# Attention operands split once and kept in DRAM, the pool half's output projection moved into attention, the mask of the row maxima done by a matmul: one transformer block on one core

## The chip, the cores and the metric

The kernel runs on one core of a Trainium2 chip. The metric is the device time of one execution in microseconds (us). The engines are TensorE (PE in the rows; its weight loads are PEld), VectorE (DVE), ScalarE (ACT), GpSimd (POOL) and SyncE (SP), which issues most DMAs. Each engine runs its own instructions in order and waits on semaphores for the others.

## The reference, cut to what matters

One block over 16 meta tokens and 1024 frames (L = 1040 positions, width 1024, all float32):

```python
n1 = _rmsnorm(h, norm1_w)
proj = n1 @ w_in                                   # q, k, v (512 each), fg (8), u (512)
q = _rmsnorm(q per head of 64, q_norm_w); k = _rmsnorm(k per head, k_norm_w)
cum_logf = cumsum(log_sigmoid(fg + b_fgate))
# 8 heads, causal: logit[t, s] = q_t.k_s / 8 + cum_logf[t] - cum_logf[s], softmax, times v
a_out = _forgetting_attention(q, k, v, cum_logf)
# pool half: per group of 128 channels, mean over a trailing window minus the value itself
p_out = einsum(pooled, w_pool) * pool_scale
h = h + concat([a_out, p_out]) @ w_out
h = h + (silu(n2 @ w_gate) * (n2 @ w_up)) @ w_down   # n2 = _rmsnorm(h); width 2816
```

## The kernel before

Everything is held transposed: channels on the 128 partitions, positions along the columns, in chunks of 512 or 346 columns, one PSUM bank of the eight for each product. To keep float32 accuracy with a fast matmul, each operand is split into a high part (a rounded copy) and a low part (the rest), and each product is three matmuls: high by high, low by high, high by low. A split is one copy on ACT and one subtraction on DVE or POOL.

The stages on TensorE are: k of the first pair of heads and the gates while x arrives; v (`v_mm`, `v_evac`); the projections of q, k and u in the order of the list `order`, the last of them q of the fourth pair of heads, whose matmuls end at 220.9 us; the four pool maps (`pool_map`, tile pm, 24 matmuls); the output projection of the pool half (16 jobs of 12 matmuls, tile o, `out_job`); attention, heads 0 to 7; the attention half of the output projection; the SwiGLU (tiles gu and d), which takes the second half of the time. The program is written out in the order in which each engine is to run it: a manual schedule, in which lambdas in queues (`later`, `bg`, `fill_q`, `mq`, `behind`) are taken out at fixed points.

What the projections leave for attention is q, k and v in float32 (tiles q32, k32, v32). For each head, `stack` makes four operands Q1, Q2, K1, K2 that hold high and low parts one above the other in two halves of 64 partitions: ACT copies the high halves, SP moves some of them to the other half of the partitions by DMA, DVE makes the low halves (L625, L629). `vsplit` splits v of one head: ACT copies, POOL subtracts (L647). Both are strung out over the steps of the head before, through `bg`.

In attention a unit is a head and one of two blocks of 512 queries. Its row maxima are taken first (`mx_steps`, tile s, lines 675 to 681): two matmuls, and a reduction on DVE; where a chunk crosses the diagonal, DVE adds the mask and reduces in one instruction (L678), which in the trace is two, the second a read of the accumulator. `mt` turns the four maxima into rows of Q2: three small DVE instructions (L693 to L695), four transposes on TensorE (tile mt, L700) and a copy on ACT. Then come 3 or 7 steps (`sp_steps`): `front` (tile st, two matmuls and, on the diagonal, a third of 128 columns with a mask, L734; then Exp twice on ACT), `mid` (the low part of the weights, on POOL or every fourth on DVE), and three steps later `back` (tile pv). For heads 1 to 3 and the first two blocks of keys, `back` multiplies unsplit float32 weights with unsplit v (tile vd, L761, `DIRECT`). `MAXN` says in which steps the next unit's maxima are taken, two at a time. `FILL` says how much of an output job is put between steps: nothing in heads 0 to 3, where all 16 pool jobs are done before, then 11/40 and 14/40 a step of the jobs that multiply the first two pairs of heads (6 matmuls each).

Of the kernel before, what the change touches and what calls it, by code (L numbers as in the profile page):

```python
# [7 lines left out]
FT = mybir.dt.float32  # L8
# [32 lines left out]
ND, DIRECT = 2, (1, 2, 3)  # L41
AGE = 2
FILL = [0] * 8 + [11 / 40] * 6 + [14 / 40] * 2
# [3 lines left out]
def block_kernel(ctx, tc, hT, n1w, w_f, w_v, w_u, w_qk, b_f, qnw, knw, w_pool, pscale, w_out, n2w, w_g, w_up, w_d, outT):  # L47
# [56 lines left out]
    maskB = const([128, 512], FT, "maskB")  # L104
    G.memset(maskB, 0.0)
    G.affine_select(maskB[:, 384:], maskB[:, 384:], pattern=[[-1, 128]], compare_op=OP.is_ge, fill=-BIG, base=0, channel_multiplier=1)
# [134 lines left out]
    v32 = [ut(1024, FT, "v32") for _ in range(5)]  # L241
# [14 lines left out]
    def v_evac(j, p):  # L256
        sz = min(128, L - 128 * j)
        A.activation(v32[j // 2][:sz, 512 * (j % 2):512 * (j % 2) + 512], p[:sz], AF.Copy, scale=rcol[:sz, j:j + 1])
# [28 lines left out]
    q32, k32 = [None] * NP, [None] * NP  # L287
    later = []

    def qk_evac(p, n, cols, w, out):  # L290
# [5 lines left out]
        def rest():  # L296
# [20 lines left out]
    k32[0] = ut(L, FT, "k32")  # L317
    for (o, n), p in zip(CH3, k0_ps):
        qk_evac(p, n, slice(o, o + n), kw, k32[0][:, o:o + n])
# [119 lines left out]
    for x, (c, i) in enumerate(order):  # L439
        if x + 2 < len(order):  # L440
            staged.append(load_w(x + 2))
        if c == "u":
            t = ut(L, FT, "u")
        else:
            t = ut(L if c == "k" else SEQ, FT, c + "32")
            (k32 if c == "k" else q32)[i] = t
        if x + 1 == len(order):
# [20 lines left out]
            for p, (o, n) in zip(pb, CHQ):  # L468
                qk_evac(p, n, slice(o, o + n), qw, t[:, o - META:o - META + n])
            break  # L470
        for o, n in CHQ if c == "q" else CH3:
# [8 lines left out]
            else:  # L480
                a = o - META if c == "q" else o
                qk_evac(p, n, slice(o, o + n), kw if c == "k" else qw, t[:, a:a + n])
# [67 lines left out]

    def fill(n):
        while n and fill_q and fill_q[0][0] <= len(split_done):
            fill_q.pop(0)[1]()
            n -= 1

    def out_job(x, b, p=None):
# [11 lines left out]
        V.tensor_tensor(h2[m][:, S], p, h2[m][:, S], op=OP.add)  # L568
# [13 lines left out]
    vhb = []  # L582
    for i in range(2):
        vhb.append([ut(192 * nj, FR, "vh").rearrange("p (j c) -> p j c", c=192) for nj in (5, 4)])
        for t, nj in zip(vhb[i], (5, 4)):
            V.tensor_copy(t[:, :, 64:128], onesf[:, None, 0:64].to_broadcast([128, nj, 64]))

    vd = ut(1024, FT, "vd").rearrange("p (i j c) -> p i j c", i=2, j=4)
    V.tensor_copy(vd[:, :, :, 64:128], onesf[:, None, 0:64].to_broadcast([128, 8, 64]).rearrange("p (i j) c -> p i j c", i=2))
# [6 lines left out]
    SE = V  # L596

    def stack(h):

        q, k = q32[h // 2], k32[h // 2]  # L600
        dma = nc.sync.dma_start
        T, B = slice(0, 64), slice(64, 128)
        R, O = (T, B) if h % 2 == 0 else (B, T)
        t = []

        def start():
            t.extend([ut(SEQ, FR, "Q1"), ut(SEQ, FR, "Q2"), ut(L, FR, "K1"), ut(L, FR, "K2")])
            dma(f(t[1])[64:66], f(KAT[0])[4 * h + 2:4 * h + 4, :SEQ])
            dma(f(t[3])[64:68], f(KAT[0])[4 * h:4 * h + 4])

        def kc(o, n):
            C = slice(o, o + n)
            A.activation(t[2][R, C], k[R, C], AF.Copy)
            dma(f(t[3])[T, C], f(t[2])[R, C])
            if h % 2:
                dma(f(t[2])[T, C], f(t[2])[B, C])

        def qc(o, n):
            C = slice(o, o + n)
            A.activation(t[0][R, C], q[R, C], AF.Copy)  # L620
            dma(f(t[0])[O, C], f(t[0])[R, C])

        def ql(o, n):
            C = slice(o, o + n)
            SE.tensor_tensor(t[1][T, C], q[R, C], f(t[0])[R, C], op=OP.subtract)  # L625

        def kl(o, n):
            C = slice(o, o + n)
            SE.tensor_tensor(t[2][B, C], k[R, C], f(t[2])[R, C], op=OP.subtract)  # L629
            if o:  # L630
                heads[h] = tuple(t)

        bg.extend([start, lambda: kc(0, 520), lambda: kc(520, 520), lambda: qc(0, 512), lambda: qc(512, 512),
                   lambda: ql(0, 512), lambda: kl(0, 520), lambda: ql(512, 512), lambda: kl(520, 520)])

    def vsplit(h):
        for j, a, e in ((0, 0, 2), (2, 0, 2), (4, 0, 1), (5, 1, 2), (6, 0, 2), (8, 0, 1)):
            def piece(j=j, a=a, e=e):
                sz = min(128, L - 128 * j)
                src = v32[j // 2].rearrange("p (a c) -> p a c", c=512)[:sz, a:e, 64 * h:64 * h + 64]  # L640
                t, J = vhb[h % 2][j // 5], slice(j % 5, j % 5 + e - a)
                if h in DIRECT and j < ND:
                    A.activation(vd[:, h % 2, j:j + 2, 0:64], src, AF.Copy)
                    if j < 2:
                        return
                A.activation(t[:sz, J, 0:64], src, AF.Copy)
                G.tensor_tensor(t[:sz, J, 128:192], src, f(t)[:sz, J, 0:64], op=OP.subtract)  # L647
            bg.append(piece)
# [10 lines left out]
    def mx_steps(h, b):  # L659
# [5 lines left out]
        for a in range(4):  # L665
# [40 lines left out]
    def sp_steps(h, b):  # L706
# [9 lines left out]
        def direct(js):  # L716
            return h in DIRECT and js[-1] < ND

        def front(js, g):

            p = ps("st")
            p32, ph = ut(512, FT, "p32"), None if direct(js) else hs(512, FR, "ph")
# [18 lines left out]
            for sz, o0, o1 in g["parts"]:  # L741
                if ph is not None:
                    A.activation(ph[:sz, o0:o1], p[:sz, o0:o1], AF.Exp)
                A.activation(p32[:sz, o0:o1], p[:sz, o0:o1], AF.Exp)  # L744

        def mid(g, sub):
            if g["ph"] is None:
                return
# [5 lines left out]
        def back(js, g):  # L754
# [3 lines left out]
            if g["ph"] is None:  # L758
                j, = js
                lo, c0 = cols_of(j)  # L760
                mm(pv[:, c0:], vd[:, h % 2, j], g["p32"][:, :512 - c0], start=j == 0, stop=False)  # L761
                return
# [63 lines left out]
    background(4)  # L826
    vsplit(0)
    for _ in range(7):
        fill(1)
        background(2)  # L830
    stack(1)
    for s in mx_steps(*units[0]):
# [639 lines left out]
```

## Time and profile before

| | us |
|---|---|
| three runs, median (lowest to highest) | 1150.87 (1149.77 to 1151.78) |
| the profiled execution: its time | 1152.16 |
| the profiled execution: its span, first to last instruction | 1150.4 |
| TensorE busy | 1118.7 |
| VectorE busy | 759.6 |
| ScalarE busy | 486.0 |
| GpSimd busy | 382.9 |
| TensorE's last matmul of the q, k and u projections starts | 220.7 |
| first step of attention starts | 277.5 |
| attention's last step ends | 453.6 |

The timeline's starts of successive matmuls tell what a matmul costs in a stream (0.23 us for 512 columns); the durations beside them overlap. Idle time of an engine is put down to the instruction that ended it. The granted clock is the share of TensorE's full clock.

### The profile page before, as it was taken

How to read it: one execution, taken by the hardware profiler on the slowest of the kernel's cores; microseconds unless marked ns; L12 is line 12 of the kernel's file. 1: busy time of each engine (PE TensorE's matmuls, PEld its weight loads, DVE VectorE, ACT ScalarE, POOL GpSimd, SP SyncE). 2: the span in 40 equal slices, each digit the busy share in tenths (PEclk: the TensorE clock that was granted, in tenths of full speed). 3: DMA queues.
4: the chain of work that ended last, by engine and by line, in shares of the span. 5: the costliest groups of instructions: out<-in, count | busy, mean ns of one | idle time of the engine just before them, and what ended most of it. 6: DMA issues, size and time to landing. Idle time of an engine off the chain costs nothing.

```text
span 1150.4 us, 14601 instructions
## 1 busy us (share of the span) xinstructions
PE 1118.7 (97%) x5251; PEld 920.8 (80%) x5251; DVE 759.6 (66%) x1237; ACT 486.0 (42%) x907; POOL 382.9 (33%) x329
## 2 busy tenths in 40 slices
PE   7999999999999999898999999999999999999998
PEld 6778899787877788676888888888888888888886
DVE  7454753774788886899554455455535569778986
ACT  7343421632778675543423232223222335344542
POOL 0011244142436565639454345434543410000000
PEclk9999999999999999998999999999999999999999
DMA  7101110251021123320322132313231479643452
GB/s 241 56 19 37 37 56 10 66 167 46 20 49 34 25 56 102 119 101 5 106 86 98 40 107 74 110 37 110 74 105 42 154 260 357 203 141 101 157 191 110
DMA packets 48407, 112.45 MB, mean 98 GB/s; under 512 B 6560, under 2 KB 9120, under 8 KB 48336
## 3 DMA queue, kind: packets, MB, share of 16 engines
q1 hardware_dynamic: 38512, 95.23, 25.3%
q10 hardware_dynamic: 9824, 16.30, 3.8%
q8 instruction: 41, 0.67, 0.2%
q14 instruction: 30, 0.25, 0.1%
HBM read 86.10 MB, written 19.92 MB: 92 GB/s over the span
## 4 chain that ended last, share of the span: by engine, by line
PE 82%; DVE 12%; ACT 3%; issue 2%; DMA 1%; POOL 0%; SPq 0%; ACTq 0%; DVEq 0%; POOLq 0%
PE gu L1140 11%; PE gu L1141 11%; PE gu L1139 11%; PE d L1381 6%; PE d L1380 6%; PE d L1379 6%; PE pj L417 3%; PE pj L418 3%; PE pj L419 3%; PE o L516 2%; PE o L518 2%; PE o L517 2%; PE v L251 2%; PE v L252 2%; PE v L253 2%
## 5 line engine op out<-in xcount | busy, mean ns | idle before, releaser
L1140 PE MATMUL gu<-cb,ws 128*128 128x512 f32 x560 | 222.2, 397 | 4.1 <-DVE ws L1130 4.1
L1141 PE MATMUL gu<-cb,ws 128*128 128x512 f32 x560 | 221.9, 396 | 0.0
L1139 PE MATMUL gu<-cb,ws 128*128 128x512 f32 x560 | 221.5, 396 | 0.0
L1130 DVE TENSOR_TENSOR ws<-wst,ws 128x512 fp32r<-128x512 f32 x120 | 97.7, 815 | 125.3 <-ACT ws L1129 125.3
L1140 PEld LDWEIGHTS gu<-cb,ws 128*128 128x128 f32 x560 | 105.9, 189 | 29.6 <-DVE ws L1130 4.5
L1129 ACT ACTIVATE ws<-wst 128x512 fp32r<-128x512 f32 x120 | 69.9, 621 | 139.5 <-POOL wst L1124 130.9
L1139 PEld LDWEIGHTS gu<-cb,ws 128*128 128x128 f32 x560 | 105.9, 189 | 25.0
L1141 PEld LDWEIGHTS gu<-cb,ws 128*128 128x128 f32 x560 | 106.0, 189 | 24.7
L1381 PE MATMUL d<-hd,wd 128*128 128x512 f32 x308 | 121.3, 394 | 0.0
L1380 PE MATMUL d<-hd,wd 128*128 128x512 f32 x308 | 121.3, 394 | 0.0
L1379 PE MATMUL d<-hd,wd 128*128 128x512 f32 x308 | 121.2, 393 | 0.0
L1153 POOL TENSOR_TENSOR e<-e,e 128x512 f32<-128x512 f32 x20 | 29.6, 1479 | 159.6 <-DVE e L1166 106.9
L752 POOL TENSOR_TENSOR pl<-p,ph 128x512 fp32r<-128x512 f32 (+4 forms) x58 | 64.5, 1124 | 45.6 <-ACT p L744 43.3
L304 POOL TENSOR_TENSOR s<-t,g 128x346 f32<-128x346 f32 (+2 forms) x20 | 21.8, 1096 | 154.3 <-ACT g L303 143.6
L417 PE MATMUL pj<-xh,wh 128*128 128x346 f32 (+2 forms) x216 | 72.9, 337 | 0.0
L418 PE MATMUL pj<-xh,wl 128*128 128x346 f32 (+2 forms) x216 | 72.9, 337 | 0.0
L419 PE MATMUL pj<-xl,wh 128*128 128x346 f32 (+2 forms) x216 | 72.8, 337 | 0.0
L1380 PEld LDWEIGHTS d<-hd,wd 128*128 128x128 f32 x308 | 57.9, 188 | 13.5
L1379 PEld LDWEIGHTS d<-hd,wd 128*128 128x128 f32 x308 | 57.9, 188 | 13.5
L1381 PEld LDWEIGHTS d<-hd,wd 128*128 128x128 f32 x308 | 57.9, 188 | 13.3
L1068 ACT ACTIVATE hd<-wst 128x512 fp32r<-128x512 f32 x77 | 48.0, 623 | 36.3 <-issue 28.9
L1069 DVE TENSOR_TENSOR hd<-wst,hd 128x512 fp32r<-128x512 f32 x77 | 52.9, 687 | 9.6 <-ACT hd L1068 9.6
(291 smaller groups left out, 2528.2 us busy)
## 6 DMA issues: line engine op xcount, KB each, us to landing
wst<-in_w_d SPq DMA_DIRECT2D x77, 256.0 KB, 2.7
wst<-in_w_g SPq DMA_DIRECT2D x22, 512.0 KB, 6.2
wst<-in_w_up SPq DMA_DIRECT2D x22, 512.0 KB, 3.4
wst<-hidd SPq DMA_DIRECT2D x22, 512.0 KB, 7.3
wst<-in_w_d SPq DMA_DIRECT2D x11, 512.0 KB, 5.0
hidd<-e ACTq DMA_DIRECT2D x20, 256.0 KB
h<-in_hT SPq DMA_DIRECT2D x8, 512.0 KB, 7.6
h2d<-h SPq DMA_DIRECT2D x16, 256.0 KB, 2.0
```

Source lines behind the costliest of these rows:

```text
L417: mm(p[:, :n], wh[:, W], xh[k][:, o:o + n], start=k == 0, stop=False)
L418: mm(p[:, :n], wl[:, W], xh[k][:, o:o + n], start=False, stop=False)
L419: mm(p[:, :n], wh[:, W], xl[k][:, o:o + n], start=False, stop=k == KT - 1)
L752: sub.tensor_tensor(pl[:sz, o0:o1], p32[:sz, o0:o1], f(ph)[:sz, o0:o1], op=OP.subtract)
L1129: A.activation(t[:, :512], src, AF.Copy)
L1130: E.tensor_tensor(t[:, 512:], src, f(t)[:, :512], op=OP.subtract)
L1139: mm(p, w[:, W], c[:, :512], start=k == 0, stop=False)
L1140: mm(p, w[:, Wl], c[:, :512], start=False, stop=False)
L1141: mm(p, w[:, W], c[:, 512:], start=False, stop=k == 3)
L1379: mm(p, w[:, W], h[:, LO], start=i == 0, stop=False)
L1380: mm(p, w[:, Wl], h[:, LO], start=False, stop=False)
L1381: mm(p, w[:, W], h[:, HI], start=False, stop=i == NPR - 1)
```

## The change

- q and k (`qk_evac`): when a chunk is finished, ACT makes its high part (`high`), a step later DVE its low part (`low`), for both heads of a pair at once; the last chunk's `low` stores both tiles in DRAM (`qkd`). `v_evac` splits v straight from PSUM, with a block of ones between high and low, and stores it (`vsd`).
- `stack` is eight DMAs on SP's queue that load Q1, Q2, K1, K2 of a head, six of them 64 partitions high (256 KB), and `vload` is three that load its v. The splits within attention, and `vd` with the unsplit products, are gone.
- The mask of the maxima is a matmul of the identity with a 128x128 mask between the other two; DVE reduces without it.
- The output jobs of the pool half: two among the maxima of the first unit, one behind them, two in a ramp before the loop, the other 11 in the steps of heads 0 to 3 (`FILL` 12/40). The attention jobs follow at 16/40 a step. The addition of a job's result to h2 (DVE) waits in `post` until the next `flush`.
- The four pool maps are interleaved with the last steps of q's and k's normalization and splits (`run_later` between them), and the maxima of the first unit come right behind them.

```diff
-FILL = [0] * 8 + [11 / 40] * 6 + [14 / 40] * 2
+RAMP = 2
+FILL = [12 / 40] * 8 + [16 / 40] * 8
...
+                def high():
+                    A.activation(th[:, C], out, AF.Copy)
+
+                    def low():
+                        V.tensor_tensor(tl[:, C], out, f(th)[:, C], op=OP.subtract)
+                        if C.stop == width:
+                            for a, x in enumerate((th, tl)):
+                                nc.sync.dma_start(qkd[name][i, a, :, :width], f(x))
+                    later.append(low)
+                later.append(high)
...
+            A.activation(t[:sz, :, 0:64], src, AF.Copy, scale=rcol[:sz, j:j + 1])
+            V.scalar_tensor_tensor(t[:sz, :, 128:192], src, rcol[:sz, j:j + 1], f(t)[:sz, :, 0:64], op0=OP.mult, op1=OP.subtract)
+            nc.sync.dma_start(vsd[j, :sz, 768 * i:768 * i + 768], f(t)[:sz].rearrange("p h c -> p (h c)"))
...
+        for t, P, src in ((Q1, T, q[0]), (K1, T, k[0]), (Q1, B, q[0]), (K1, B, k[1]), (Q2, T, q[1]), (K2, T, k[0])):
+            dma(f(t)[P], src)
...
                     mm(p[:, :n], Q1[:, T], K1[:, o:o + n], start=True, stop=False)
+                    if last:
+                        mm(p[:, n - 128:n], ident, maskB, start=False, stop=False)
                     mm(p[:, :n], Q2[0:66, T], K2[0:66, o:o + n], start=False, stop=True)
-                    if last:
-                        V.tensor_tensor_reduce(p[:, :n], p[:, :n], maskB[:, 512 - n:], 1.0, -3e38, OP.add, OP.max,
-                                               accum_out=mp[:, a, c:c + 1])
-                    else:
-                        V.tensor_reduce(mp[:, a, c:c + 1], p[:, :n], op=OP.max, axis=AX.X)
+                    V.tensor_reduce(mp[:, a, c:c + 1], p[:, :n], op=OP.max, axis=AX.X)
...
+    stack(0)
+    vload(0)
     for g in (3, 2, 1, 0):
         pool_map(g)
-    stack(0)
-    for x in range(2):
-        fill(1)
-        background(3)
         now, later[:] = later[:], []
         run_later(now)
+    s0 = mx_steps(*units[0])
+    for x, s in enumerate(s0):
+        s()
+        if x % 2:
+            fill(1)
+            now, later[:] = later[:], []
+            run_later(now)
...
-    for _ in range(5):
+    for _ in range(RAMP):
         fill(1)
-        max_next(1)
-    max_next(2)
+        max_next(2)
```

ScalarE at the pool maps, before. mph is the high part of a pool map, g the reciprocal root of the last q chunks, K1 and Q1 head 0's operands:

```order
L501 ACTIVATE mph_325_1950<-pm_327_1952,psc_101 128x512
L501 ACTIVATE mph_325_1950<-pm_328_1958,psc_101 128x512
L501 ACTIVATE mph_329_1964<-pm_331_1966,psc_101 128x512
L501 ACTIVATE mph_329_1964<-pm_332_1972,psc_101 128x512
L501 ACTIVATE mph_333_1978<-pm_335_1980,psc_101 128x512
L501 ACTIVATE mph_333_1978<-pm_336_1986,psc_101 128x512
L501 ACTIVATE mph_337_1992<-pm_339_1994,psc_101 128x512
L501 ACTIVATE mph_337_1992<-pm_340_2000,psc_101 128x512
L545 ACTIVATE wo_344_2024<-wos_324_1948 128x512
L613 ACTIVATE K1_347_2029<-k32_67_482 64x520 x2
L302 ACTIVATE g_351_2041<-t_350_2040 128x512
L303 ACTIVATE g_351_2041<-g_351_2041 128x512
```

The same place in the changed kernel; kh and qh are the high parts of the last k and q:

```order
L529 ACTIVATE mph_346_2077<-pm_349_2085,psc_103 128x512
L330 ACTIVATE kh_284_1814<-k32_283_1813 128x346
L320 ACTIVATE g_352_2097<-t_351_2096 128x512
L321 ACTIVATE g_352_2097<-g_352_2097 128x512
L320 ACTIVATE g_356_2107<-t_355_2106 128x512
L321 ACTIVATE g_356_2107<-g_356_2107 128x512
L529 ACTIVATE mph_358_2113<-pm_360_2115,psc_103 128x512
L529 ACTIVATE mph_358_2113<-pm_361_2121,psc_103 128x512
L529 ACTIVATE mph_362_2136<-pm_364_2138,psc_103 128x512
L529 ACTIVATE mph_362_2136<-pm_365_2144,psc_103 128x512
L330 ACTIVATE qh_309_1938<-q32_308_1937 128x512 x2
L529 ACTIVATE mph_366_2152<-pm_368_2154,psc_103 128x512
```

The first map's parts stand where they stood; behind them now come the four instructions on g, and the last map's parts stand behind qh, which reads the finished q.

TensorE at the end of the same place in the changed kernel, from the last pool map on; s is a maximum of unit (0, 0), o the first output job:

```order
L528 MATMUL pm_369_2160<-wl_327_2028,wh_322_2001 128x512
L666 MATMUL s_371_2172<-K1_344_2064,Q1_342_2062 128x144
L668 MATMUL s_371_2172<-maskB_86,ident_69 128x128
L669 MATMUL s_371_2172<-K2_345_2065,Q2_343_2063 128x144
L666 MATMUL s_372_2177<-K1_344_2064,Q1_342_2062 128x272
L668 MATMUL s_372_2177<-maskB_86,ident_69 128x128
L669 MATMUL s_372_2177<-K2_345_2065,Q2_343_2063 128x272
L544 MATMUL o_375_2186<-mph_346_2077,wo_339_2055 128x512
L545 MATMUL o_375_2186<-mph_346_2077,wo_339_2055 128x512
L546 MATMUL o_375_2186<-mpl_347_2078,wo_339_2055 128x512
```

Before, the first o stood right behind the last pm, with the second q chunk's sums of squares (ss) behind it:

```order
L500 MATMUL pm_340_2000<-wl_309_1910,wh_304_1883 128x512
L516 MATMUL o_343_2010<-mph_325_1950,wo_322_1943 128x512
L517 MATMUL o_343_2010<-mph_325_1950,wo_322_1943 128x512
L518 MATMUL o_343_2010<-mpl_326_1951,wo_322_1943 128x512
L516 MATMUL o_343_2010<-mph_329_1964,wo_322_1943 128x512
```

In both kernels the last three matmuls of an o job read the last map's mph and mpl. In the changed kernel the ss matmuls stand between the first map and the second.

## Rows read from the trace of the kernel before

**Rows 1.** The page: busy time, share of the span and instructions by engine.
```profile
PE 1118.7 (97%) x5251; PEld 920.8 (80%) x5251; DVE 759.6 (66%) x1237; ACT 486.0 (42%) x907; POOL 382.9 (33%) x329
```
**Rows 2.** Stretches of one head each: length; PE, PEld, DVE, ACT, POOL busy; clock; DMA.
```profile
300.65:320.60 19.95, 19.28 (x113) 15.66 (x111) 17.15 (x41) 16.40 (x38) 9.49 (x12) 1.00 0.15 35
...
409.16:432.80 23.64, 21.90 (x129) 18.26 (x127) 21.71 (x46) 17.19 (x39) 14.92 (x19) 1.00 0.26 72
```
**Rows 3.** PE groups, 276.4 to 453.6: count | busy, mean ns | idle before, releasers.
```profile
L732 PE MATMUL st<-Q,K 128*128 128x512 f32 (+4 forms) x112 | 42.0, 375 | 0.7 <-DVE a L791 0.4 <-DVE mp L681 0.2
...
L675 PE MATMUL s<-K,Q 128*128 128x456 f32 (+6 forms) x103 | 34.0, 336 | 2.3 <-DVE a L791 1.8 <-DVE mp L678 0.4 <-ACT p L744 0.2
...
L700 PE MATMUL mt<-ident,Mc 128*68 128x128 f32 x60 | 7.0, 239 | 5.9 <-DVE Mc L695 3.2 <-DVE mp L663 1.1 <-ACT p L744 0.9
```
**Rows 4.** PE timeline, start and duration: a pair without mask; a pv triple, a masked pair.
```profile
287.37 0.39 PE L732 MATMUL st<-Q,K 128*128 128x512 f32 x1
...
287.83 0.35 PE L675 MATMUL s<-K,Q 128*128 128x400 f32 x1
...
316.11 0.40 PE L770 MATMUL pv<-ph,vh 128*128 128x512 f32 x1
...
316.82 0.39 PE L732 MATMUL st<-Q,K 128*128 128x512 f32 x1
317.05 0.21 PE L734 MATMUL st<-maskA,ident 128*128 128x112 f32 x1
317.10 0.45 PE L735 MATMUL st<-Q,K 68*128 68x512 f32 x1
317.39 0.32 PE L675 MATMUL s<-K,Q 128*128 128x346 f32 x1
```
**Rows 5.** PE timeline: an unsplit product (vd), the pair behind it, and what follows.
```profile
303.64 1.02 PE L761 MATMUL pv<-p,vd 128*128 128x512 f32 x2
...
304.97 0.23 PE L675 MATMUL s<-K,Q 128*128 128x144 f32 x1
```
**Rows 6.** DVE, ACT and POOL groups by form, 220.7 to 256 us: the pool maps.
```profile
L502 DVE SCALAR_TENSOR_TENSOR mpl<-pm,psc,mph 128x512 fp32r<-128x512 f32 x8 | 5.3, 736 | 0.0
L307 DVE SCALAR_TENSOR_TENSOR s<-s,g 128x512 f32<-128x512 f32 x2 | 2.5, 1254 | 0.0
...
L309 DVE SCALAR_TENSOR_TENSOR q<-pj,qw,g 128x512 f32<-128x512 f32 x2 | 1.5, 752 | 0.1
...
L501 ACT ACTIVATE mph<-pm,psc 128x512 fp32r<-128x512 f32 x8 | 5.0, 722 | 1.0 <-PE pm L500 1.0
...
L304 POOL TENSOR_TENSOR s<-t,g 128x512 f32<-128x512 f32 x2 | 2.6, 1304 | 3.0 <-ACT g L303 3.0
```
**Rows 7.** Timeline at the pool maps: DVE's last sum of squares, PE's maps.
```profile
222.51 0.69 DVE L294 TENSOR_TENSOR sql<-sq,sqh 128x512 fp32r<-128x512 f32 x1 [0.29 <-ACT sq L293]
...
220.91 0.39 PE L498 MATMUL pm<-wh,wh 128*128 128x512 f32 x1
...
226.43 0.50 PE L498 MATMUL pm<-wh,wh 128*128 128x512 f32 x1 [1.19 <-DVE mpl L502]
```
**Rows 8.** PE timeline: the longest wait in attention, and matmuls soon after it.
```profile
281.79 0.43 PE L700 MATMUL mt<-ident,Mc 128*68 128x128 f32 x4 [2.40 <-DVE Mc L695]
...
284.14 0.63 PE L771 MATMUL pv<-ph,vh 128*64 128x512 f32 x1
284.56 0.63 PE L772 MATMUL pv<-pl,vh 128*128 128x512 f32 x1
```
**Rows 9.** DVE groups by form, 276.4 to 453.6 us: work that the change removes.
```profile
L629 DVE TENSOR_TENSOR K<-k,K 64x520 fp32r<-64x520 f32 x12 | 10.3, 856 | 2.0 <-DMA K<-K 1.8
...
L625 DVE TENSOR_TENSOR Q<-q,Q 64x512 fp32r<-64x512 f32 x12 | 9.7, 809 | 4.9 <-ACT Q L620 4.6
...
L678 DVE DVE_READ_ACCUMULATOR2_ANT mp<- 128x1 f32 x58 | 8.0, 138 | 0.1
```
**Rows 10.** DMA issues: size of each, median us from issue to landing.
```profile
res<-h2d SPq DMA_DIRECT2D x16, 256.0 KB, 2.8
```

More of the change, by code (lines that the diff above doesn't have):

```diff
@@ L238, in block_kernel @@
         A.activation(fgT[:16, o:o + n], fg_ps[c][:16, :n], AF.Copy)
-    v32 = [ut(1024, FT, "v32") for _ in range(5)]
+    vst, vsd = [], DR.tile([ST, 128, 192 * NH], FT, name="vsd")
     rcol = const([128, ST], FT, "rcol")
@@ L284, in block_kernel, with qk_tile, qk_evac @@
         V.tensor_scalar(qrow[:, o:o + n], p[:, :n], 1.0 / D, EPS, op0=OP.mult, op1=OP.add)
-    q32, k32 = [None] * NP, [None] * NP
+    qkd = {c: DR.tile([NP, 2, 128, L], FT, name=f"{c}d") for c in "qk"}
     later = []
-    def qk_evac(p, n, cols, w, out):
+    def qk_tile(c, i):
+        n = L if c == "k" else SEQ
+        return c, i, n, ut(n, FT, c + "32"), ut(n, FR, c + "h"), ut(n, FR, c + "l")
+    def qk_evac(p, n, cols, w, tile, C):
+        name, i, width, t32, th, tl = tile
+        out = t32[:, C]
         h, l, s = hs(n, FR, "sqh"), hs(n, FR, "sql"), hs(n, FT, "sq")
@@ L444, in block_kernel @@
         else:
-            t = ut(L if c == "k" else SEQ, FT, c + "32")
-            (k32 if c == "k" else q32)[i] = t
+            t = qk_tile(c, i)
         if x + 1 == len(order):
@@ L481, in block_kernel @@
                 a = o - META if c == "q" else o
-                qk_evac(p, n, slice(o, o + n), kw if c == "k" else qw, t[:, a:a + n])
+                qk_evac(p, n, slice(o, o + n), kw if c == "k" else qw, t, slice(a, a + n))
             run_later(now)
@@ L549, in block_kernel, with flush @@
     wo = {}
+    post = []
+    def flush():
+        while post:
+            post.pop(0)()
     def fill(n):
         while n and fill_q and fill_q[0][0] <= len(split_done):
+            flush()
             fill_q.pop(0)[1]()
@@ L578, in out_fill @@
             fill_q.extend([(need, lambda x=x: out_job(x, 0)), (need, lambda x=x: out_job(x, 1))])
[L582 to L589, printed above, removed]
+    vhb = [[ut(192 * nj, FR, "vh").rearrange("p (j c) -> p j c", c=192) for nj in (5, 4)] for _ in range(2)]
     Mc = [const([128, 4, 68], FR, f"Mc{i}") for i in range(2)]
@@ L594, in block_kernel @@
     heads = {}
-    SE = V
     def stack(h):
-        q, k = q32[h // 2], k32[h // 2]
         dma = nc.sync.dma_start
         T, B = slice(0, 64), slice(64, 128)
[L603 to L648, printed above, removed]
+        R = (T, B)[h % 2]
@@ new lines, in stack, with vload @@
+        Q1, Q2, K1, K2 = heads[h] = ut(SEQ, FR, "Q1"), ut(SEQ, FR, "Q2"), ut(L, FR, "K1"), ut(L, FR, "K2")
+        q, k = [[qkd[c][h // 2, a, R, :n] for a in range(2)] for c, n in (("q", SEQ), ("k", L))]
+        for t, P, src in ((Q1, T, q[0]), (K1, T, k[0]), (Q1, B, q[0]), (K1, B, k[1]), (Q2, T, q[1]), (K2, T, k[0])):
+            dma(f(t)[P], src)
+        dma(f(Q2)[64:66], f(KAT[0])[4 * h + 2:4 * h + 4, :SEQ])
+        dma(f(K2)[64:68], f(KAT[0])[4 * h:4 * h + 4])
+    def vload(h):
+        for t, j, n, sz in ((0, 0, 5, 128), (1, 5, 3, 128), (1, 8, 1, 16)):
+            o = j - 5 * t
+            nc.sync.dma_start(f(vhb[h % 2][t])[:sz, o:o + n], vsd[j:j + n, :sz, 192 * h:192 * h + 192].rearrange("j p c -> p j c"))
@@ L714, in cols_of @@
             return lo, max(lo, 0)
-        def direct(js):
-            return h in DIRECT and js[-1] < ND
         def front(js, g):
             p = ps("st")
-            p32, ph = ut(512, FT, "p32"), None if direct(js) else hs(512, FR, "ph")
+            p32, ph = ut(512, FT, "p32"), hs(512, FR, "ph")
             g["p32"], g["ph"], g["parts"] = p32, ph, []
@@ L741, in front @@
             for sz, o0, o1 in g["parts"]:
-                if ph is not None:
-                    A.activation(ph[:sz, o0:o1], p[:sz, o0:o1], AF.Exp)
+                A.activation(ph[:sz, o0:o1], p[:sz, o0:o1], AF.Exp)
                 A.activation(p32[:sz, o0:o1], p[:sz, o0:o1], AF.Exp)
         def mid(g, sub):
-            if g["ph"] is None:
-                return
             ph, pl, p32 = g["ph"], hs(512, FR, "pl"), g["p32"]
@@ L757, in back @@
             pv = state["pv"]
[L758 to L762, printed above, removed]
             ph, pl = g["P"]
@@ L817, in block_kernel @@
     wo[1] = out_load(1)
+    stack(0)
+    vload(0)
     for g in (3, 2, 1, 0):
         pool_map(g)
-    stack(0)
-    for x in range(2):
-        fill(1)
-        background(3)
         now, later[:] = later[:], []
         run_later(now)
[L826 to L830, printed above, removed]
+    s0 = mx_steps(*units[0])
[5 more added lines that the diff above has]
+            run_later(now)
+    while later:
+        now, later[:] = later[:], []
+        run_later(now)
     stack(1)
-    for s in mx_steps(*units[0]):
-        s()
-        background(2)
     fin = mt(*units[0])
-    fill(2)
+    fill(1)
     fin()
```

29 lines of the change are left out of this document (19 added, 10 removed).

## The prediction

> **What bounds the kernel now.** The page comes first: TensorE is busy 97% of the span, VectorE 66%, nobody else half [rows 1]. So the time is the list of matmuls plus the places where TensorE stands still, and an edit counts only if it changes one of these two. Next come the stretches of single heads, because the page's shares are means over stages. A head without output jobs takes 19.95 us, of which TensorE works 19.28 and DVE 17.15; one with attention jobs takes 23.64, with 21.90 and 21.71 [rows 2]. DVE is near its limit there, but TensorE's loss is small: over the whole of attention (277 to 454 us) its idle time stands at three lines, the steps' first matmul (0.7), the maxima (2.3) and the transposes mt (5.9), 8.9 us together [rows 3]. The timeline then gives the price of matmuls: 0.23 us from start to start for 512 columns, a pair in 0.46 (287.37 to 287.83) [rows 4]. The durations beside the starts overlap and are not used.
>
> **The mask as a matmul (adds).** Each of the 16 units has four maxima that cross the diagonal: 64 matmuls of 128 columns more. The trace of before has the same operation in the diagonal steps. The masked pair runs from 316.82 to 317.39, 0.57 us, the plain pair 0.46 [rows 4]: 0.11 each, 64 x 0.11 = **+7.0**. Low end: between the mask's start and its successor's lie only 0.05 (317.05 to 317.10) [rows 4], 64 x 0.05 = 3.2. Both rows show one event; I take 0.11, since it counts what comes back later, when the successor's own columns have run. In exchange DVE loses the second instruction of each such reduction, the read of the accumulator: 58 of these, 8.0 us [rows 9], about 1.0 a head.
> The rows show 0.11 for the third matmul of a group of mixed size. The Trainium skill, "TensorE: Matmul & The Clock Gate", section "Back-to-back issue gap", gives about 81 ns for each matmul of 128 columns in a stream in which every matmul loads its weights. By that figure the term would be an estimated 64 x 0.081 = 5.2 and the sum 1.8 lower; the sum keeps the row.
>
> **Unsplit products go.** Twelve `vd` matmuls become triples with twelve more Exps and mids. One with a pair behind it takes 303.64 to 304.97, 1.33 us [rows 5]; less the pair's 0.46 that is 0.87. A split triple takes 316.11 to 316.82, 0.71 [rows 4]. Nine have 512 columns, three 400: 9 x 0.16 + 3 x 0.13 = **-1.8**. The extra Exps lie on ACT, 16.40 of 19.95 us busy in these heads [rows 2]; four more per head at about 0.6 bring it to 18.8, but without the copies for the split it falls by more than that. Ends: -1.0 and -2.5.
>
> **q's tail between the pool maps (moves).** Before, TensorE's first pm starts at 220.91 and waits only once, 1.19 us for a bank that an mpl frees, at 226.43 [rows 7]; sixteen o jobs behind it cover the whole normalization of the last q. After, only three o jobs stand before attention's first step, and the order on ACT puts the last map's two mph behind qh, which needs the finished q. I follow that chain with durations of before: 0.63 for an ACT instruction of 128x512 (5.0/8), 0.67 for mpl (5.3/8), 1.3 for POOL's product, and for DVE's s, g, q of one chunk three at 0.75 [rows 6]. DVE ends its last sql at 222.51 + 0.69 = 223.2 [rows 7]; two small Mc casts, mpl twice, kl, t twice: 226.8. ACT's four instructions on g end at 228.7, its four mph of the next two maps at 231.3. POOL is done with the second chunk by 230.0. DVE does mpl twice and kl, then six instructions on s, g, q: 231.2 + 4.5 = 235.7. ACT's qh ends at 236.4, the first half of the last mph at 237.0, DVE's first half of mpl at 237.8. Three matmuls of the first o job stand behind these, so that job ends at about 238.1. Without waits it would end at 220.9 + 24 pm (5.6) + ss (0.9) + two short masked maxima (0.7) + 12 matmuls (2.8) = 230.9. The wait is 7.2; before, this place lost about 1.4, so **+5.8** remain. What hides less than I think: nothing stands between on TensorE, since every matmul that follows is in order behind that o job. Ends: the chain may run shorter where ACT and DVE overlap more closely (one chunk's q done early lets the first half of qh go), then the net is 0; with s at its slower mean, 1254 ns [rows 6], and a POOL that competes with DVE, it is +9.
>
> **The clock after a wait.** The longest wait of attention, 2.40 us at 281.79, is followed 2.4 us later by matmuls that start 0.42 us apart (284.14, 284.56) instead of 0.23 [rows 8]. Some six matmuls are so, 0.2 each: **+1.2** for the longer wait at the maps; ends 0 and +3 (all of 3 us at half speed).
>
> **Waits of attention.** Per head DVE loses two instructions of each kind of low part, and the 12 of each in this stretch are those of six heads: (10.3 + 9.7)/6 = 3.3 us; the accumulator reads are another 1.0 [rows 9]. ACT and POOL lose their copies and subtractions of v. In return DVE gets about three additions to h2 of 0.7 in heads 0 to 3, which makes some 15 busy of about 27 us, as the 11 pool jobs (2.8 us of TensorE each) stretch these heads; and four attention jobs a head of 1.4 us instead of three, in heads 4 to 7. With more matmuls between a maximum and its mt, and a freer DVE, most of 8.9 us of waits [rows 3] should go. One remains by the order: at the first unit's change mt stands directly behind the next maxima, as at 281.79, 2.40 [rows 8]. I take **-5.0**. Ends: 0 (the three small instructions before mt are a chain of fixed length) and -11.5 (all idle time and the slowed matmuls).
>
> **Edits at nothing.** The splits of q, k and v: some 12 us each of ACT and DVE more during the projections, where DVE is the busiest with about three quarters; TensorE's matmuls there stand back to back, so the cover is the projections' own 12 matmuls a chunk; 0 to +1. The stores to DRAM (SP) are read long after. A head's loads (eight transfers, six of 256 KB, and three for v) replace SP's moves between the halves. A load of 256 KB lands 2.8 us after its issue [rows 10]; one after the other the six take 16.8 us, in a head of 20 to 28, and they are issued a head ahead, without a wait of TensorE: 0. Four attention jobs fewer are left for the end of attention, where they cover the second normalization: 0 to +2. Nothing is gained by moving the pool jobs as such: they are the same matmuls.
>
> **Sum.** The profiled execution took 1152.16, span 1150.4, with 1.8 around it. 1152.16 + 7.0 - 1.8 + 5.8 + 1.2 - 5.0 = 1159.4. The runs' median lies 1.3 below that execution, so the forecast is **1158**.
>
> **Rivals.** *B, the maps hide and the waits vanish.* If the first o's wait stays under 3 us (net +2, no clock loss) and all waits of attention go (-11.5), the time is 1150.9 + 7.0 - 1.8 + 2 - 11.5 = 1146.6. For it: DVE's share in heads 0 to 3 falls to some 60%. Against: the order on ACT. It decides from the point where the last mph is done before 234 instead of 237.7. *C, it nets out:* the waits go as far as idle time reaches (-8.9), the maps cost +3.5, no slowed clock: 1150.9 + 7.0 - 1.8 + 3.5 - 8.9 = 1150.7, no change. *D, head loads late.* The half loads share the queue with weights and h2's tiles; if a head's Q and K come after the last step of the head before, because the tiles' buffers are freed only then, six heads wait about 1.5 us each (half of one landing of 2.8 us [rows 10]): 1158 + 9 = 1167. Against: DMA is busy 15 to 26% of a head [rows 2]. It decides from the point where a load is issued less than 17 us before its first use.
> No transfer from DRAM to half of the partitions stands in the rows. The Trainium skill, "DMA: Bandwidth & Descriptors", section "Rules for kernel authors", says that two transfers to disjoint halves of the partitions serialize, and advises one of all 128. That is a case for D, which takes the six one after the other already; the trace here neither confirms nor denies it.
>
> **How the numbers follow.** Forecast 0.46, B 0.18, C 0.18, D 0.18. A measurement of this kernel can tell some 0.2%, 2.3 us, from no change. Faster is B, 0.18; same is C, 0.18; slower the rest, 0.64. The forecast's own terms reach from 1151 (the maps and the clock at 0) to 1166 (the maps at +9, nothing gained in attention). The range goes from there down to B, 1146.5 to 1166; about half of B and half of D lie outside, 0.18.
>
> **What would show it.** In the profile of the changed kernel: the o job's third last matmul with an idle time of 6 us or more put down to ACT mph, and qh just ahead of it on ACT; the masked s groups 0.11 longer than the plain ones; idle time of mt and s in attention down from 8.2 to 3 or 4; no DMA as releaser of s or st. The prediction is wrong if the first o job passes without that wait, if the mask's start to start is nearer to 0.05, or if a DMA ends idle time in front of a head's first matmul.

## The result, and the profile after

The changed kernel takes 1160.24 us (median of four runs, 1158.36 to 1161.63) against 1150.98 (1149.77 to 1151.78): 1.008 times as long, 95% interval 1.0061 to 1.0100. The forecast was 1158 in a range of 1146.5 to 1166. The profiled execution took 1161.34, with a span of 1159.6. TensorE is as full as before [rows 1], but of a longer list:

```profile
PE 1127.5 (97%) x5327; PEld 932.9 (80%) x5327; DVE 747.6 (64%) x1185; ACT 478.1 (41%) x868; POOL 373.9 (32%) x292
```

The starts of a stage's first matmul in the two timelines give the lengths of the stages (us). The pool jobs moved, so the maps, the output jobs and attention are one stage:

| stage, by first matmuls | before | after | difference |
|---|---|---|---|
| start to first pj | 89.49 | 90.00 | +0.5 |
| projections, to first pm | 131.42 | 131.33 | -0.1 |
| maps, output jobs, attention, to the first job of the last two pairs of heads (wc) | 238.39 | 246.11 | +7.7 |
| those jobs, to the first SwiGLU matmul | 27.39 | 30.28 | +2.9 |
| SwiGLU, first half (gu) | 446.00 | 444.12 | -1.9 |
| SwiGLU, second half (d) | 214.07 | 214.04 | 0.0 |

The first stage, in which the inputs arrive, varies between 87.1 and 90.0 in the profiles shown below, and gu between 444.1 and 446.0; so stages are compared, and differences of 2 us in the total of one profile are not read.

**The maps.** TensorE's timeline there (start, duration, in brackets the idle time and what ended it), to be held against [rows 7]:

```profile
228.53 0.39 PE L528 MATMUL pm<-wl,wh 128*128 128x512 f32 x1
231.15 0.33 PE L666 MATMUL s<-K,Q 128*128 128x144 f32 x1 [2.22 <-DVE mpl L530]
...
232.09 0.34 PE L669 MATMUL s<-K,Q 66*128 66x272 f32 x1
234.44 0.77 PE L544 MATMUL o<-mph,wo 128*128 128x512 f32 x1 [2.00 <-DVE q L327]
235.00 0.63 PE L545 MATMUL o<-mph,wo 128*128 128x512 f32 x1
235.43 0.63 PE L546 MATMUL o<-mpl,wo 128*128 128x512 f32 x1
...
239.27 0.63 PE L546 MATMUL o<-mpl,wo 128*128 128x512 f32 x1
239.69 0.54 PE L666 MATMUL s<-K,Q 128*128 128x400 f32 x1
```

Two waits, 2.22 and 2.00 us, and behind them a job of 12 matmuls that takes 234.44 to 239.69, 5.25 us in place of 12 x 0.23 = 2.8. The releasers are instructions that empty a PSUM bank: mpl of the second map, and q's product. The second map's bank is held that long because its mph stands on ACT behind the four instructions on g, which wait for DVE:

```profile
227.25 0.63 ACT L320 ACTIVATE g<-t 128x512 f32<-128x512 f32 x1 [2.30 <-DVE t L319]
...
229.64 2.41 ACT L529 ACTIVATE mph<-pm,psc 128x512 fp32r<-128x512 f32 x4
...
236.43 0.63 ACT L330 ACTIVATE qh<-q 128x512 fp32r<-128x512 f32 x1 [1.48 <-DVE q L327]
236.97 1.25 ACT L529 ACTIVATE mph<-pm,psc 128x512 fp32r<-128x512 f32 x2
```

The granted clock in two stretches (length, PE busy, clock, DMA share, GB/s) is the lower of its two levels, 1.2 GHz, through that job:

```profile
235.00:239.50 4.50, 4.50 (x12) 0.50 0.29 117
241.00:246.00 5.00, 5.00 (x25) 0.95 0.80 258
```

**Attention.** The rows that answer to [rows 3], and the view of the tile mt (idle time before it, by what ended it):

```profile
L721 PE MATMUL st<-Q,K 68*128 68x512 f32 (+4 forms) x112 | 40.3, 360 | 0.4 <-ACT Q L690 0.2
...
L666 PE MATMUL s<-K,Q 128*128 128x392 f32 (+6 forms) x104 | 34.5, 332 | 0.3 <-DVE a L769 0.2
```
```profile
L689 PE MATMUL mt<-ident,Mc x64: 221/223/319, 246.6 to 444.6; 128*68 128x128 f32 x64
its engine sat idle before it (us, times) until:
  DVE Mc L684: 3.6, 3
```

Idle time at these lines is 4.3 us where it was 8.9, and the maxima's own wait fell from 2.3 to 0.3. Most of what is left is one place, the answer to [rows 8]:

```profile
258.23 0.37 PE L669 MATMUL s<-K,Q 66*128 66x346 f32 x1
261.25 0.64 PE L689 MATMUL mt<-ident,Mc 128*68 128x128 f32 x4 [2.65 <-DVE Mc L684]
261.68 0.74 PE L718 MATMUL st<-Q,K 128*128 128x512 f32 x1
262.56 0.80 PE L721 MATMUL st<-Q,K 68*128 68x512 f32 x1
263.15 0.63 PE L748 MATMUL pv<-ph,vh 128*128 128x512 f32 x1
```

The wait is about as long as before (2.65 against 2.40), but a dozen matmuls behind it run at the lower clock (0.43 apart until 267.4), where before it was some six. DVE, which makes Mc, was held up there: an addition to h2 waited for the load of an h2 tile, and five reductions stood behind it:

```profile
257.54 0.69 DVE L603 TENSOR_TENSOR h<-o,h 128x512 f32<-128x512 f32 x1 [2.74 <-DMA h<-in_hT]
258.15 2.44 DVE L670 TENSOR_REDUCE mp<-s 128x1 f32<-128x456 f32 x5
```

From 246 to 258 us the DMA engines are busy all the time (shares of 1.01 to 1.06), with head 1's loads among what they move. That these loads delay the tile is likely and not shown. In e9 (below), where no addition waits for a load there, the transposes wait 1.41; e9 differs in more than this.

**The mask.** A plain maximum of 346 columns, and the masked one behind it:

```profile
312.38 0.32 PE L666 MATMUL s<-K,Q 128*128 128x346 f32 x1
312.54 0.33 PE L669 MATMUL s<-K,Q 66*128 66x346 f32 x1
312.70 0.33 PE L666 MATMUL s<-K,Q 128*128 128x346 f32 x1
312.86 0.22 PE L668 MATMUL s<-maskB,ident 128*128 128x128 f32 x1
312.92 0.37 PE L669 MATMUL s<-K,Q 66*128 66x346 f32 x1
313.13 0.40 PE L748 MATMUL pv<-ph,vh 128*128 128x512 f32 x1
```

0.32 and 0.43 us: the mask costs 0.11, although its successor starts only 0.06 behind it. The same groups in e2 (below), where DVE masks, are shorter by 0.10 to 0.11 (medians) in all eight widths: 64 x 0.11 = 7.0 us. At 456 columns the like has to be held against the like. The masked group, which follows a matmul of 16 columns, takes 0.62 (310.16 to 310.78 in the changed kernel), but the same group without a mask takes 0.51 there (308.83 to 309.34 in e2), where the other group of 456 columns takes 0.42:

```profile
310.16 0.46 PE L666 MATMUL s<-K,Q 128*128 128x456 f32 x1
...
310.78 0.32 PE L666 MATMUL s<-K,Q 128*128 128x348 f32 x1
```
```profile
308.83 0.46 PE L664 MATMUL s<-K,Q 128*128 128x456 f32 x1
...
309.34 0.33 PE L664 MATMUL s<-K,Q 128*128 128x348 f32 x1
```

**The end of attention.** The second normalization's first matmul, which waited 1.24 us before, the first row, waits 3.88 after:

```profile
475.98 0.50 PE L879 MATMUL n<-wh,ones 128*128 128x512 f32 x1 [1.24 <-ACT wh L126]
```
```profile
482.60 0.40 PE L546 MATMUL o<-ml,wc 128*128 128x512 f32 x1
486.88 0.80 PE L857 MATMUL n<-wh,ones 128*128 128x512 f32 x1 [3.88 <-ACT wh L129]
```

### The profile page after: what moved, and what is told of

Read it like the earlier page. It is cut to its first block, busy times and chain, and to the rows that moved or that the text cites. A ratio compares the mean times of both kernels' runs of the same rounds, so it can differ in the third digit from the quotient of the medians.

```text
span 1159.6 us, 14738 instructions
## 1 busy us (share of the span) xinstructions
PE 1127.5 (97%) x5327; PEld 932.9 (80%) x5327; DVE 747.6 (64%) x1185; ACT 478.1 (41%) x868; POOL 373.9 (32%) x292
## 4 chain that ended last, share of the span: by engine, by line
PE 83%; DVE 8%; DMA 3%; ACT 2%; issue 2%; POOL 1%; SPq 0%; ACTq 0%; POOLq 0%; DVEq 0%
PE gu L1118 10%; PE gu L1117 10%; PE gu L1116 10%; PE d L1358 6%; PE d L1360 6%; PE d L1359 6%; PE pj L447 3%; PE pj L448 3%; PE pj L446 3%; PE o L544 2%; PE st L721 2%; PE o L545 2%; PE o L546 2%; PE v L254 2%; PE v L255 2%
## 5 line engine op out<-in xcount | busy, mean ns | idle before, releaser
L735 POOL TENSOR_TENSOR pl<-p,ph 128x512 fp32r<-128x512 f32 (+4 forms) x66 | 72.6, 1112 | 56.9 <-ACT p L729 47.9
L670 DVE TENSOR_REDUCE mp<-s 128x1 f32<-128x144 f32 (+6 forms) x112 | 52.5, 504 | 30.3 <-PE s L669 28.4
L728 ACT ACTIVATE ph<-st 128x512 fp32r<-128x512 f32 (+4 forms) x88 | 46.4, 528 | 58.4 <-PE st L721 55.2
```

The source lines that it names most:

```text
L735: sub.tensor_tensor(pl[:sz, o0:o1], p32[:sz, o0:o1], f(ph)[:sz, o0:o1], op=OP.subtract)
```

## The experiments

Each was timed against the kernel before on the same chip. Differences between two of them are differences of medians; by the ratios they come out within 1 us of that.

**e1_maps: the maps unbroken** (after, one part undone).
```diff
     for g in (3, 2, 1, 0):
         pool_map(g)
-        now, later[:] = later[:], []
-        run_later(now)
```


> The changed kernel with one part undone: the four pool maps run without a break, and q's last steps come behind the first output job. Theory (the broken-up maps cost most of the loss: two waits for PSUM banks of 2.4 and 2.2 us and a slowed clock over the first o job, 2.6 us, against 1.4 us before): 1160.2 less 7 to 8 us, 1152 to 1153, and the stretch from the first pm to the first step of attention shorter by as much. Rival (q's steps only wait later, at the first units' transposes, or a slowed clock remains): 1157 or more, with a new wait of over 2 us between 228 and 262 us.

1160.77 us, ratio 1.0084 (1.0071 to 1.0096): nothing gained, the theory fell. The two waits at the maps are gone, and one of 5.12 us stands at the first unit's transposes, with the slowed clock behind it:

```profile
237.61 0.39 PE L546 MATMUL o<-mpl,wo 128*128 128x512 f32 x1
243.12 0.61 PE L689 MATMUL mt<-ident,Mc 128*68 128x128 f32 x4 [5.12 <-DVE Mc L684]
243.53 0.74 PE L544 MATMUL o<-mph,wo 128*128 128x512 f32 x1
```

DVE's timeline of the same kernel says why. q's steps (s, g, q of two chunks, ql) stand ahead of Mc:

```profile
234.69 1.77 DVE L325 SCALAR_TENSOR_TENSOR s<-s,g 128x512 f32<-128x512 f32 x1
...
239.34 0.75 DVE L327 SCALAR_TENSOR_TENSOR q<-pj,qw,g 128x512 f32<-128x512 f32 x1
...
240.34 1.28 DVE L333 TENSOR_TENSOR ql<-q,qh 128x512 fp32r<-128x512 f32 x2
241.54 0.15 DVE L682 TENSOR_REDUCE mx<-mp 128x4 f32<-128x12 f32 x1
...
242.81 0.17 DVE L684 SCALAR_TENSOR_TENSOR Mc<-mx,Mc 128x4 fp32r<-128x4 f32 x1
```

So a second theory: the cost is the length of q's chain in front of work that TensorE waits for, wherever the maps stand.

**e9_qtail: maps unbroken, q's steps behind the first unit's transposes** on every engine.
```diff
     for g in (3, 2, 1, 0):
         pool_map(g)
-        now, later[:] = later[:], []
-        run_later(now)
-    s0 = mx_steps(*units[0])
-    for x, s in enumerate(s0):
+    for s in mx_steps(*units[0]):
         s()
-        if x % 2:
-            fill(1)
-            now, later[:] = later[:], []
-            run_later(now)
-    while later:
-        now, later[:] = later[:], []
-        run_later(now)
     stack(1)
     fin = mt(*units[0])
     fill(1)
     fin()
+    for _ in range(2):
+        now, later[:] = later[:], []
+        run_later(now)
+        fill(1)
+    while later:
+        now, later[:] = later[:], []
+        run_later(now)
```


> The changed kernel with the pool maps unbroken and the last q's steps moved behind the first unit's transposes, on every engine, under the second, third and fourth output job. Theory (not the maps but the chain of q's last steps is what TensorE waits for: with the maps unbroken it stood ahead of the first unit's transposes on DVE, and the wait of 5.3 us came back there): about 7 us less between the first pm and the first step of attention, 1153. Rival (three output jobs are too short a cover for the chain wherever it stands, and the first step or the maxima of unit (0, 1) wait for it): 1158 or more, with a wait of over 2 us between 230 and 262 us.

1149.88 us, ratio 0.9985 (0.9976 to 0.9993): 10.4 us below the changed kernel, the same matmuls in another order. First pm to first step takes 25.66 us in place of 32.69 (e1: 32.90); the rest comes from the wait before unit (0, 1)'s transposes, 1.41 in place of 2.65, and fewer matmuls at the lower clock. The transposes now follow their output job at once, and DVE has Mc done before q's steps begin:

```profile
230.44 0.40 PE L546 MATMUL o<-mpl,wo 128*128 128x512 f32 x1
230.68 0.41 PE L689 MATMUL mt<-ident,Mc 128*68 128x128 f32 x4
230.92 0.45 PE L316 MATMUL ss<-sqh,bones 128*128 128x512 f32 x1
```
```profile
230.11 0.17 DVE L684 SCALAR_TENSOR_TENSOR Mc<-mx,Mc 128x4 fp32r<-128x4 f32 x1
...
235.14 1.76 DVE L325 SCALAR_TENSOR_TENSOR s<-s,g 128x512 f32<-128x512 f32 x1 [1.19 <-POOL s L322]
```

**e2_dvemask: the mask back on DVE** (after, one part undone).
```diff
...
-                    if last:
-                        mm(p[:, n - 128:n], ident, maskB, start=False, stop=False)
...
+                    if last:
+                        V.tensor_tensor_reduce(p[:, :n], p[:, :n], maskB[:, 512 - n:], 1.0, -3e38, OP.add, OP.max,
+                                               accum_out=mp[:, a, c:c + 1])
+                    else:
+                        V.tensor_reduce(mp[:, a, c:c + 1], p[:, :n], op=OP.max, axis=AX.X)
```


> The changed kernel with the mask of the maxima back on DVE (add and reduce in one instruction) and no mask matmul. Theory (a mask matmul costs TensorE 0.11 us and hides nothing): 64 x 0.11 = 7.0 us less TensorE work, about 1 us of it given back in waits for DVE: 1154. Rival 1 (0.05 to 0.06 each): 1156.5 to 1157. Rival 2 (the mask matmul pays for itself, because DVE's longer reductions delay the maxima): 1160 or more.

1155.30 us, ratio 1.0031 (1.0020 to 1.0043): 4.9 lower, all of it in the stage of attention (maps to wc 240.4 in place of 246.1). Between the theory and rival 1: the groups show the full 7.0, of which the stage gives back 5.7 (and 6.0 in e12 against e9, below: 230.3 and 236.3). Heads 1 to 3 are shorter by 0.82 to 0.93 us each, the price of their eight masks (0.88). The rest goes mostly in head 0, where a wait of 1.59 us for ACT's Exp (before 258.55) is new: ACT had stood until 256.76 for the load of an output weight that it copies ahead of its first Exps. The mask need not be the cause, since e5, whose mask is a matmul, waits 1.28 at the same place, behind the same copy (256.91; in the changed kernel it comes at 256.12).

**e3_before_mm: the mask matmul alone in the kernel before.**
```diff
...
+                    if last:
+                        mm(p[:, n - 128:n], ident, maskB, start=False, stop=False)
...
```
(with the plain reduction for every maximum)

> The kernel before with one part added: the mask of the maxima as a matmul, DVE reduces without it. Theory (0.11 each, with about 1 us fewer waits for DVE): 1151.0 + 6 = 1157. Rival 1 (0.05 to 0.06 each): 1154. Rival 2 (DVE's relief in heads 4 to 7 pays for it): 1151 or less.

1154.34 us, ratio 1.0028 (1.0017 to 1.0040): +3.1, rival 1's number, but not its reason. Here too the groups cost 0.11 more in every width, 7.0 in all; DVE is nearer to its limit in this kernel [rows 2], and with its relief the idle time at the three lines of [rows 3] falls from 8.9 to 5.4 us: 7.0 - 3.5 = 3.5.

**e6_nodirect: the unsplit products alone taken out of the kernel before.**
```diff
-ND, DIRECT = 2, (1, 2, 3)
+ND, DIRECT = 2, ()
```


> The kernel before with one part of the change: no unsplit products, heads 1 to 3 split all weights and v as the other heads do. Theory (12 triples in place of 12 unsplit products, 1.8 us of TensorE less, and the copies and Exps lie beside it): 1151.2 - 1.8 = 1149.4. Rival (in this kernel ACT and DVE are so full in heads 1 to 3, 16.4 and 17.2 of 19.95 us, that the extra Exps and low parts bring waits): 1151 to 1153.

1156.41 us, ratio 1.0040 (1.0027 to 1.0052): 4.5 us slower, beyond both expectations. The maxima wait 6.0 us in attention in place of 2.3 [rows 3], 5.0 of it for DVE's end of a unit (a), the instruction that has read the last unit's pv from its bank:

```profile
L675 PE MATMUL s<-K,Q 128*128 128x456 f32 (+6 forms) x102 | 34.7, 345 | 6.0 <-DVE a L791 5.0 <-ACT p L744 0.5 <-DMA Q<-Q 0.3
```
```profile
312.93 0.34 PE L676 MATMUL s<-K,Q 66*128 66x392 f32 x1
314.91 0.45 PE L675 MATMUL s<-K,Q 128*128 128x456 f32 x1 [1.64 <-DVE a L791]
```

**e4_ramp4: four output jobs and eight maxima ahead of attention.**
```diff
-RAMP = 2
+RAMP = 4
```


> The changed kernel with four output jobs and eight maxima ahead of the first step of attention in place of two and four (two of the jobs come from the steps of heads 0 to 3). Theory (the longest wait of attention, 2.85 us before the transposes of unit (0, 1), another 0.65 behind it and 2.7 us of slowed clock, stands there because three maxima of that unit are left over at its start): these go, 1160.2 - 5 = 1155. Rival (the wait is that of the chain from maxima to transposes and only moves, or the two jobs are missed in heads 0 to 3): 1159 to 1161.

1159.26 us (1156.99 to 1161.87), ratio 1.0066 (1.0051 to 1.0081). The wait before unit (0, 1)'s transposes stays, 2.28 us, though only its last maximum comes behind the first step's matmuls: DVE's three small instructions come behind other reductions and an addition to h2. The rival, then; the total can't be told from the changed kernel's.

**e5_tail: three or four attention jobs left for the end.**
```diff
-FILL = [12 / 40] * 8 + [16 / 40] * 8
+FILL = [12 / 40] * 8 + [13 / 40] * 8
```


> The changed kernel with 13/40 in place of 16/40 of an output job per step in heads 4 to 7, so that three or four attention jobs are left for the end of attention, as in the kernel before. Theory (the stage from the first job of the last two pairs of heads to the first matmul of the SwiGLU takes 30.28 us in place of 27.39, because these jobs' additions now queue on DVE behind the end of the last unit, and the second normalization's matmul waits 4.05 in place of 1.41 us): this stage back to 27.4 to 27.8 and the total 2.5 to 3 lower, 1157.5. Rival (attention gains from the jobs that it has, and loses it again): the stage is shorter, attention longer, the total 1159.5 to 1161.

1160.37 us, ratio 1.0072 (1.0058 to 1.0086). The rival: the last stage falls from 30.28 to 27.73 as expected, and the stage before it grows by 3.9. New waits stand in the last head, in which fewer jobs cover the transposes' copy on ACT (below) and the low parts on POOL (1.1 us). Another of 1.3 stands at unit (0, 1), in a head that this edit doesn't reach. The wait for the copy:

```profile
445.05 0.50 PE L718 MATMUL st<-Q,K 128*128 128x512 f32 x1
447.09 0.50 PE L721 MATMUL st<-Q,K 68*128 68x512 f32 x1 [1.54 <-ACT Q L690]
```

**e13_poolfirst: e9 with all 16 pool jobs ahead of attention.**
```diff
-RAMP = 2
-FILL = [12 / 40] * 8 + [16 / 40] * 8
+RAMP = 13
+FILL = [0] * 8 + [16 / 40] * 8
...
-    for _ in range(RAMP):
+    for x in range(RAMP):
         fill(1)
-        max_next(2)
+        if x > 5:
+            max_next(1)
```


> The changed kernel with q's last steps behind the first unit's transposes, and all 16 pool jobs ahead of the first step of attention, none in heads 0 to 3 (13 in the ramp, with seven maxima of unit (0, 1) among the last of them). Theory (the pool jobs are the same matmuls wherever they stand, but inside attention they give DVE and ACT time: without them heads 0 to 3 get their waits back, some 4 to 6 us in place of the 2 they have): 1152 to 1154, against 1149.9 with the jobs inside. Rival (with the splits gone, heads 0 to 3 don't need the jobs as cover): 1149 to 1150.5.

1154.24 us (12 runs, 1150.36 to 1158.34), ratio 1.0020 (1.0007 to 1.0033) where e9 had 0.9985: about 4 us. Heads 0 to 3 take 82.95 us; e9's 110.65 less its 11 jobs of 2.78 are 80.07. So in this profile heads 0 to 3 lose some 3 us without the jobs. How much of that is the jobs' cover is open: the profile is of the slowest run and holds another wait of 1.65 at head 0's loads, and three of the 12 runs, at 1150.4 to 1150.9, lie among e9's (1149.3 to 1152.1).

**e10_best, e12_two, e11_ramp: combinations.** e12 is e9 with e2's edit; e10 is e12 with e5's; e11 is e12 with this:
```diff
-    step, share = 0, 0.0
+    step, share = 0, 1 - FILL[0]
...
-    for _ in range(RAMP):
+    for x in range(RAMP):
         fill(1)
-        max_next(2)
+        max_next(4 - x)
```


> The changed kernel with three parts altered at once: q's last steps behind the first unit's transposes, 13/40 in heads 4 to 7, and the mask of the maxima back on DVE. Theory (the three losses are separate): 1160.5 - 7 - 2.8 - 5 = 1145.7, below the kernel before. Rival (the losses overlap, a freer stretch only moves the wait to the next): 1150 or more.

> The changed kernel with two parts altered: q's last steps behind the first unit's transposes, and the mask of the maxima back on DVE; the jobs in heads 4 to 7 stay at 16/40. Theory (leaving jobs for the end gave nothing, since attention lost what the end gained; the mask costs the same with and without the late q steps): 1149.9 - 5 = 1145, below the run with 13/40 (1148.1). Rival (with the q steps gone from the front, the mask on DVE delays the maxima more): 1148 to 1150.

> As the run before, and unit (0, 1)'s maxima are taken in threes and fours under the two output jobs ahead of attention, with one job of heads 0 to 3 put behind the first step. Theory (the wait before unit (0, 1)'s transposes, 1.6 to 1.75 us, 0.6 behind it and 1.6 of slowed clock stand there because three maxima are left over at its start): 2 to 3.5 us lower than that run, 1142. Rival (the chain from the last maximum to the transposes is late anyway, the wait moves by a few matmuls): within 1 us of that run.

e10: 1148.06 us (1143.51 to 1150.64), ratio 0.9967 (0.9951 to 0.9983), between its theory and its rival. e12: 1143.95, ratio 0.9939 (0.9925 to 0.9952), below both kernels: the two losses are separate (1160.2 - 10.4 - 4.9 = 1144.9), and e5's edit, worth nothing alone, costs 3 to 4 us here. e11: 1144.01, ratio 0.9943 (0.9929 to 0.9957): the wait at unit (0, 1) is gone, and others stand before 354.19 (1.74, where e12 has 0.55) and before 430.56 (1.59). The rival's number holds, and not its reason: the wait did not move by a few matmuls, the time is lost elsewhere.

## Why the prediction was right, and where it was not

- **Direction and size.** The forecast sum was +7.2 against the profiled execution of before; measured +9.2 there and +9.3 by the medians. Of its terms two held in size, the mask and the maps; the others were off or stand by themselves in no run, partly against each other.
- **The mask, +7.0.** Right as a price: 0.11 on TensorE each, 7.0 in all. The low end from the mask's own start interval is refuted: that interval is 0.06, which the prediction had named as a sign against itself, but what counts is the whole group. DVE's relief, which the prediction put into the waits, pays a part back: undoing the mask alone is worth 4.9 here, and adding it alone costs 3.1 before. The Trainium skill's page "TensorE: Matmul & The Clock Gate", section "Back-to-back issue gap", gives about 81 ns for such a matmul in a stream. These groups measure 100 to 110, so the row was the better guide.
- **The pool maps, +5.8 and +1.2.** Right in size, wrong in where, so the close number is in part luck. First pm to the end of the first output job takes 221.34 to 239.69, 18.35 us; without waits it was put at 10.0, so 8.35 are lost, 1.4 before: +7.0, the sum of the two terms. The chain itself came 0.7 us later than worked out (the last qh ends at 237.06, put at 236.4). But the step said that the job's last three matmuls wait for the last map's mph behind qh, and named 6 us of idle time there as its sign. They wait for nothing; TensorE had stood already, for two PSUM banks: the second map's, whose mph stands behind g on ACT (2.22), and q's own (2.00). The lower clock makes 2.5 us of the loss and not 1.2. By e1 the order of the maps on ACT, on which the step rested, is not what the time hangs on: with it undone the same time is lost at the transposes. By e9 the cause is that q's chain stands in front of attention's first work. Behind the first unit's transposes, with as few output jobs beside it, it brings no wait but perhaps a part of the 1.41 us at unit (0, 1), for this q belongs to the fourth pair of heads and is needed late. The step laid the loss to missing cover (it counted three jobs ahead of the first step; there are five, three of them ahead of the first unit's transposes) and drew the wait from one pair of instructions. No run left the chain in its place and gave it more cover.
- **The unsplit products, -1.8.** The price of the matmuls was read rightly, but no run isolates the term in the changed kernel. The step leaned on ACT's copies going at the same time and looked at ACT alone. e6 shows what the products cost without that: alone, in the kernel before, 4.5 us, and the waits are for DVE. That they don't cost that here goes with the splits that left attention: in one head of the changed kernel (head 2; columns as in [rows 2]) DVE works 15.0 of 27.7 us, where it worked 17.15 of 19.95 [rows 2]. The pool jobs, which stretch that head, are not the reason: in e13, without them, head 1 has DVE busy for 12.59 of 19.38. The two parts have to be priced as one, as the step did for ACT only.

```profile
311.80:339.54 27.74, 27.74 (x162) 24.01 (x160) 15.00 (x34) 15.70 (x31) 13.40 (x13) 0.95 0.53 140
```

- **Waits of attention, -5.0.** Idle time fell by 4.6 at the lines named, at mt and s from 8.2 to 3.9, as foreseen; with the slowed matmuls behind the one wait that was said to stay it is about 3. That wait did stay. "Nothing is gained by moving the pool jobs as such" looks too narrow: without the jobs inside, e13 is about 4 us slower than e9, though not in every run.
- **The end of attention, 0 to +2.** It is +2.9: the additions of the last jobs queue on DVE behind the end of the last unit. Leaving jobs for the end, as e5 does, brings this stage back and loses the same inside attention.
- **The heads' loads, 0.** Held after, where no DMA ends a wait of s or st. The half loads land 6.6 (K) and 7.8 us (Q) after their issue (medians) and not 2.8 [rows 10], each behind others of its row; "DMA: Bandwidth & Descriptors", section "Rules for kernel authors", in the Trainium skill had warned that such halves serialize. No run separates that from their waiting in one queue. They are issued a head ahead, which hides it. In e1, e9, e10, e11, e12 and e13, where attention's first maxima come earlier, head 0's loads end a wait of 0.4 to 1.7 us: rival D's mechanism, at one place. By way of DVE a load does reach TensorE in the changed kernel too: the late h2 tile ahead of unit (0, 1)'s transposes (above), of the kind that D put in one queue with the half loads.
- **SwiGLU's first half, -1.9,** no step foresaw. In both kernels TensorE waits 4.1 us there, once, for split weights (ws; before 540.21, and before 551.23 after the change), and fewer matmuls run at the lower clock behind that wait. Since this stage varies as much among the other profiles, no cause is claimed. Nor do the terms add up closer than about 1.5 us.

## What to carry to other kernels

When filler work is moved away from a long serial chain, ask what else covers that chain: the wait follows the chain to whatever stands behind it in any engine's queue, and reordering its neighbours only moves it. If its product is needed late, put the chain behind the work that the bound engine waits for. A small instruction moved from a busy engine to the one that sets the time costs its full price there (0.11 us x 64), and the relief pays only a part back. Two parts of a change that load and relieve the same engine (unsplit products out, splits out) are to be priced together, on every engine that they touch: one alone was 4.5 us slower.

## What the runs showed of the hardware

- A wait can cost more than itself: behind one of 2.00 us, 12 matmuls ran at a granted clock of 0.50, and the wait of 2.65 us before 261.25 was followed by 12 more, another 2.4 us (12 x 0.2). Not every wait does so: behind one of 1.64 us (before 314.91 in e6) the matmuls of 512 columns start 0.23 to 0.24 apart.
- A granted clock of 0.95 in a busy stretch isn't slower work: the changed kernel's profile records a mean of 0.938 against 0.991, and its projections take 131.33 us against 131.42.
- A matmul of 128 columns between two others of a group costs 0.10 to 0.11 us in all eight widths, although its successor starts 0.06 us behind it. The price has to be taken from group to group, and from the same place in both kernels: at 456 columns the place alone makes a difference of 0.09.
